# A two-layer hybrid decoder: packed weights and regrouped tiles in the last output projection, norm factors turned without a copy

## The chip, the cores and the metric

One core of one Trainium2 chip. The metric is the device time of one execution in microseconds (us), the median of three runs. The profile comes from one more execution of the same program, whose own time is given beside its span.

## The reference, cut to what matters

One sequence of 1024 positions and width 1024, a memory of 256 positions, float32 throughout. Two layers, each with one gated mixer: layer 0 is latent attention (12 heads), layer 1 an RWKV-7 recurrence (24 heads of 64), and in both four more heads attend to the memory.

```python
for layer in (mla, rwkv7):
    h = rmsnorm(x, norm_g)
    u = h @ w_in                        # queries, keys, gates ... of all heads
    mix = mixer(u)                      # 12 * 128 features
    mem_mix = memory_attention(q, *split(rmsnorm(mem, mem_norm_g) @ w_mem_kv))
    y = concat(mix, mem_mix) * silu(gate)          # 2048 features
    x = x + y @ w_out                   # the output projection
return rmsnorm(x, final_g)
```

## The kernel before

Everything lies transposed: features in the 128 partitions, positions in the columns, cut in two halves of T = 512 columns (`hf` 0 and 1). A feature tile is 128 features by 512 positions; x has 8, the gated y of a layer 16 (k 0 to 11 from the mixer, 12 to 15 from the memory heads).

Each float32 product is made of three: an operand is split into a rounded high part and the rest. For weights, `weights()` loads up to 512 columns into `wr`, ACT casts them to `wh` (L152) and DVE subtracts to get `wl` (L153); `mm3()` then issues `wh` by `yh` (L160), `wh` by `yl` (L161) and `wl` by `yh` (L162). A column of 128 weights serves one such triple. `wr`, `wh` and `wl` rotate through four buffers each; nearly all transfers are issued by SP, in order.

**Norms.** `squares()` collects the sum of squares over feature tiles in `sqa`: ACT squares (L183), DVE adds (L184). `rstd_rows()` sums over the partitions on PE (L206), which leaves one sum per position, positions in the partitions. DVE computes one over the root with whole numbers and three Newton steps on small tiles `n` (L208, L192 to L197), and a copy spreads each factor over 128 columns of `rw` (L211). `rstd_spread()` transposes `rw` on PE (L218), which puts the factor of each position into every partition, and ACT copies this from PSUM to `rstd` (L220), by which DVE multiplies the tiles. Eleven norms go this way: one for each half of x and for the two latent vectors of layer 0, one for the memory, one for each half of x at the start of layer 1 (`begin`), and the final one for each half (`finish`).

**Order.** The kernel is written with generators; `interleave()` mixes the steps of several. At build time a scheduler then sets each engine's order from its own estimates and from the buffers that are free, so an edit at one place can move instructions at others. Layer 1 runs 24 items (12 pairs of heads by two halves) through five stages; the last stage, `norm`, gives a gated y tile. The tables F0 and F1 say at which step how many tiles of the output projection of a half are woven in (`finish(0)`, `finish(1)`).

**The last output projection** is `out_proj` of layer 1 and the second half, called from `finish(1)`. It takes the y tiles in six groups, (12, 16), (0, 4), (4, 8), (8, 10), (10, 11), (11, 12), since the tiles 8 to 11 come last from the recurrence. In the first three groups each output tile m takes the group's product in PSUM and adds it to `xr` (L389). From the group (8, 10) on (`held=3`) the six output tiles m = 0 to 5 keep one PSUM bank each, in which the three last groups add up; each group loads the weights of each m by itself (256, 128 and 128 columns), 18 loads. For m = 6 and 7 nothing is done in these groups until the last, where each loads 512 columns and takes four y tiles, 12 matmuls, in the banks `c` and `y`. Behind the last group come the additions, squares, the final norm, eight multiplications (L928) and eight stores.

The y tile k=11 ends in `norm`: ACT copies it to `yT`, DVE normalises each head over its features (`m`, then `yT`, L1262), PE transposes back to a bank `y` (L1266), DVE makes `rk` and the gated `sg` (L1267, L1268), and ACT and DVE split it to `yh` and `yl` (L128, L129).

**The opening.** x is loaded, normalised and projected; `pos` gives, by `ang`, the tables of sine and cosine; the memory is normalised (`mn`), split (`mh`, `ml`) and projected to keys `mk` (copied by ACT, L271) and values. All share PE with the projections of layer 0.

## Time and profile before

| | us |
|---|---|
| runs: median (lowest to highest) | 2519.84 (2515.22 to 2521.16) |
| the profiled execution, its own time | 2510.56 |
| its span | 2508.8 |
| PE busy | 2420.2 (96%) |
| DVE busy | 1936.4 (77%) |
| ACT busy | 1375.7 (55%) |
| mean granted TensorE clock | 0.996 of full |

A busy time counts an instruction from start to end, and matmuls overlap, so what a matmul costs in a row of them is read from start to start. An idle time in brackets is time of that engine ahead of the instruction; it costs something only where the chain to the end runs through it. [...]

### The profile page before, as it was taken

How to read it: one execution, taken by the hardware profiler on the slowest of the kernel's cores; microseconds unless marked ns; L12 is line 12 of the kernel's file. 1: busy time of each engine (PE TensorE's matmuls, PEld its weight loads, DVE VectorE, ACT ScalarE, POOL GpSimd, SP SyncE). 2: the span in 40 equal slices, each digit the busy share in tenths (PEclk: the TensorE clock that was granted, in tenths of full speed). 3: DMA queues.
4: the chain of work that ended last, by engine and by line, in shares of the span. 5: the costliest groups of instructions: out<-in, count | busy, mean ns of one | idle time of the engine just before them, and what ended most of it. 6: DMA issues, size and time to landing. Idle time of an engine off the chain costs nothing.

```text
span 2508.8 us, 39875 instructions
## 1 busy us (share of the span) xinstructions
PE 2420.2 (96%) x13298; PEld 1996.1 (80%) x13298; DVE 1936.4 (77%) x5750; ACT 1375.7 (55%) x2973; POOL 55.1 (2%) x158
## 2 busy tenths in 40 slices
PE   8899999999999999999999999999999999999997
PEld 6698888888888778877778777777777777788785
DVE  7756455877787766698888888888888898786975
ACT  6445345554555334565665666666666665654542
POOL 0000000000000100000000000000000000000000
PEclk9999999999999999999999999999999999999998
DMA  5352222111112443422122222322222123222332
GB/s 178 111 171 85 76 80 74 51 56 54 49 64 68 159 168 136 143 78 76 58 73 79 80 79 78 100 82 77 79 81 80 62 84 118 87 94 98 118 137 70
DMA packets 165982, 231.45 MB, mean 92 GB/s; under 512 B 46096, under 2 KB 67984, under 8 KB 165776
## 3 DMA queue, kind: packets, MB, share of 16 engines
q1 hardware_dynamic: 165776, 228.90, 27.7%
q8 instruction: 105, 1.72, 0.3%
q14 instruction: 101, 0.83, 0.1%
HBM read 187.66 MB, written 37.49 MB: 90 GB/s over the span
## 4 chain that ended last, share of the span: by engine, by line
PE 75%; DVE 15%; ACT 6%; issue 3%; DMA 2%; SPq 0%; DVEq 0%; ACTq 0%
PE mm L160 15%; PE mm L161 15%; PE mm L162 15%; PE a L1085 3%; PE c L1218 2%; DVE tmp L1136 2%; PE pt L724 2%; DVE U L1140 2%; PE c L1221 1%; PE y L1225 1%; PE po L160 1%; PE po L161 1%; PE y L1224 1%; DVE wl L153 1%; PE po L162 1%
## 5 line engine op out<-in xcount | busy, mean ns | idle before, releaser
L152 ACT CAST wh<-wr 128x512 fp32r<-128x512 f32 (+3 forms) x500 | 299.0, 600 | 436.0 <-PE mm L161 381.0
L153 DVE TENSOR_TENSOR wl<-wr,wh 128x512 fp32r<-128x512 f32 (+3 forms) x500 | 329.6, 661 | 132.3 <-ACT wh L152 113.0
L160 PE MATMUL mm<-xnh,wh 128*128 128x512 f32 x912 | 373.9, 410 | 0.8 <-DVE qml L134 0.6
L161 PE MATMUL mm<-xnl,wh 128*128 128x512 f32 x912 | 371.2, 407 | 0.0
L162 PE MATMUL mm<-xnh,wl 128*128 128x512 f32 x912 | 369.7, 406 | 0.0
L160 PE MATMUL mm<-yh,wh 128*128 128x512 f32 x492 | 198.9, 404 | 4.3 <-DVE xr L389 4.1
L162 PE MATMUL mm<-yh,wl 128*128 128x512 f32 x492 | 196.8, 400 | 0.0
L160 PEld LDWEIGHTS mm<-xnh,wh 128*128 128x128 f32 x912 | 172.1, 189 | 30.5 <-issue 2.6
L161 PE MATMUL mm<-yl,wh 128*128 128x512 f32 x492 | 195.5, 397 | 0.0
L161 PEld LDWEIGHTS mm<-xnl,wh 128*128 128x128 f32 x912 | 172.3, 189 | 27.2 <-issue 1.4
L162 PEld LDWEIGHTS mm<-xnh,wl 128*128 128x128 f32 x912 | 172.1, 189 | 27.3 <-issue 1.0
L160 PE MATMUL mm<-xh,wh 128*128 128x512 f32 x416 | 165.2, 398 | 7.6 <-ACT xh L438 7.6
L161 PE MATMUL mm<-xl,wh 128*128 128x512 f32 x416 | 164.9, 396 | 0.6 <-DVE xl L439 0.6
L1140 DVE TENSOR_TENSOR U<-U,tmp 128x60 f32<-128x60 f32 (+24 forms) x744 | 155.9, 210 | 12.3 <-PE b L1171 0.5
L1136 DVE TENSOR_TENSOR tmp<-As,U 128x60 f32<-128x60 f32 (+24 forms) x744 | 155.6, 209 | 12.1
L162 PE MATMUL mm<-xh,wl 128*128 128x512 f32 x416 | 164.3, 395 | 0.0
L1232 ACT ACTIVATE sc<-S,f 128x128 f32<-128x128 f32 x168 | 67.4, 401 | 169.5 <-DVE S L1233 155.9
L302 ACT ACTIVATE p<-b,sm 128x512 f32<-128x512 f32 (+2 forms) x144 | 82.8, 579 | 107.3 <-DVE sm L299 82.2
L389 DVE TENSOR_TENSOR xr<-mm,xr 128x512 f32<-128x512 f32 x123 | 84.5, 688 | 67.1 <-PE mm L162 65.2
L160 PEld LDWEIGHTS mm<-yh,wh 128*128 128x128 f32 x492 | 92.7, 188 | 22.6 <-DVE xr L389 3.5
L297 DVE TENSOR_REDUCE sm<-b 128x1 f32<-128x256 f32 (+1 forms) x176 | 90.3, 527 | 24.8 <-PE b L686 10.1
L162 PEld LDWEIGHTS mm<-yh,wl 128*128 128x128 f32 x492 | 92.7, 188 | 17.0 <-issue 0.2
(361 smaller groups left out, 5968.8 us busy)
## 6 DMA issues: line engine op xcount, KB each, us to landing
wr<-in_wu_dram SPq DMA_DIRECT2D x292, 256.0 KB, 2.7
wr<-in_wo_dram SPq DMA_DIRECT2D x122, 256.0 KB, 2.6
yr<-y SPq DMA_DIRECT2D x60, 256.0 KB, 3.8
As<-sysd SPq DMA_DIRECT2D x24, 512.0 KB, 4.3
y<-y SPq DMA_DIRECT2D x32, 256.0 KB, 2.0
y<-sg SPq DMA_DIRECT2D x32, 256.0 KB, 2.0
g<-u SPq DMA_DIRECT2D x24, 256.0 KB, 2.3
gt<-g SPq DMA_DIRECT2D x24, 256.0 KB, 2.8
```

What stands on the lines that cost most here:

```text
L152: nc.scalar.copy(hi[:, :n], raw[:, :n])
L153: nc.vector.tensor_sub(lo[:, :n], raw[:, :n], hi[:, :n].bitcast(F32))
L160: mm(ps, a[0], b[0], start=start, stop=False)
L161: mm(ps, a[0], b[1], start=False, stop=False)
L162: mm(ps, a[1], b[0], start=False, stop=stop)
L297: nc.vector.tensor_reduce(sm[:, i : i + 1], ps[:, :own], AX.X, ALU.max, negate=True)
L302: nc.scalar.activation(p[:, :own], ps[:, :own], AF.Exp, bias=sm[:, 0:1], accum_out=sm[:, 2 + i : 3 + i])
L389: nc.vector.tensor_add(xs[m][:], ps[:], xs[m][:])
L1085: mm(ps[:, j * 256 : j * 256 + 256], BK[c // 4][:, c % 4, :], AR[:, c, :], start=True, stop=True)
L1136: E.tensor_tensor(out=tmp[:, 0:u, 0:n], in0=As[:, 0:u, u : u + 1].broadcast_to([P, u, n]), in1=U[:, u : u + 1, i0:8].broadcast_to([P, u, n ...
L1140: E.tensor_tensor(out=U[:, 0:u, i0:8], in0=U[:, 0:u, i0:8], in1=tmp[:, 0:u, 0:n], op=ALU.add)
L1232: ACT.activation(sc[:], cur, AF.Copy, scale=fc)
```

## The change

Three things. In the held groups `shared()` packs the weights of several output tiles into one buffer of 512 columns: two tiles for the group (8, 10), four for (10, 11) and (11, 12), with a transfer for each tile and one cast and one difference for the pack. Tiles 6 and 7 join the held groups: tile 6 begins at the group (10, 11) and tile 7 at (11, 12), each with its own load for the y tiles that came before (`before()`). `rstd_rows()` returns the small tile `n` itself, without the copy `rw`, and `rstd_spread()` transposes from one of its columns, read 128 times; with `out=False`, as in the final norm of the second half, it returns the PSUM bank, and the multiplications (now L953) read that.

```diff
@@ -38,7 +38,7 @@
 B0, S0 = 12, (10, 10)
 
 F0 = ((20, 6), (21, 2), (22, 4), (23, 10), (24, 11), (25, 11))
-F1 = ((24, 1), (25, 13), (26, 17), (27, 6))
+F1 = ((24, 1), (25, 13), (26, 17), (27, 7))
 ATT_SCALE = float(192.0 ** -0.5)
 MEM_SCALE = float(128.0 ** -0.5)
 NEG = -1.0e30
@@ -207,15 +207,15 @@
         q = self.smp.tile([P, 24], F32, tag="n", bufs=2, name=self.name("n"))
         nc.vector.tensor_scalar(q[:, 8 : 8 + n], ps[:, :n], 1.0 / width, EPS_N, ALU.mult, ALU.add)
         self.rsqrt(q, n)
-        w = self.g(s="rw")
-        nc.vector.tensor_copy(w[:, :N].rearrange("p (i t) -> p i t", t=P), q[:, 0:n:2].unsqueeze(2).broadcast_to([P, n // 2, P]))
-        return w
+        return q
 
     def rstd_spread(self, w, aux, N=T, out=None):
 
         ps = aux()
         for i in range(0, N, P):
-            self.nc.tensor.transpose(ps[:, i : i + P], w[:, i : i + P], self.ident)
+            self.nc.tensor.transpose(ps[:, i : i + P], w[:, i // 64 : i // 64 + 1].broadcast_to([P, P]), self.ident)
+        if out is False:
+            return ps
         r = out or self.g(s="rstd")
         self.nc.scalar.copy(r[:, :N], ps[:, :N])
         return r
@@ -342,7 +342,7 @@
 
 
         nc, A = self.nc, self.A
-        xs, acc, ys, kept, last = [], None, {}, [], len(groups) - 1
+        xs, acc, ys, kept, last = [], None, {}, {}, len(groups) - 1
 
         def load(g):
             raw = []
@@ -357,6 +357,32 @@
                 self.split(hi[:], lo[:], t[:])
                 ys[k] = (hi[:], lo[:])
 
+        def before(m, first, k0):
+
+            o, n = m % 2 * T + first % 4 * P, (k0 - first) * P
+            ws = self.weights(A["wo"][l, first // 4, m // 2][:, o : o + n], n)
+            self.gemm(kept[m][:], ws, [ys[k] for k in range(first, k0)], k0 - first, end=False)
+
+        pack = {}
+
+        def shared(m, k0, k1):
+
+            n = (k1 - k0) * P
+            per = min(4, T // n)
+            if (k0, m // per) not in pack:
+                raw = self.wp.tile([P, T], F32, tag="wr", name=self.name("wr"))
+                hi, lo = (self.ws.tile([P, T], F32R, tag=t, name=self.name(t)) for t in ("wh", "wl"))
+                for j in range(per):
+                    q = m // per * per + j
+                    o = q % 2 * T + k0 % 4 * P
+                    nc.sync.dma_start(raw[:, j * n : j * n + n], A["wo"][l, k0 // 4, q // 2][:, o : o + n])
+                nc.scalar.copy(hi[:], raw[:])
+                nc.vector.tensor_sub(lo[:], raw[:], hi[:].bitcast(F32))
+                pack[k0, m // per] = hi, lo
+            hi, lo = pack[k0, m // per]
+            o = m % per * n
+            return [(hi[:, o : o + n], lo[:, o : o + n])]
+
         for g, (k0, k1) in enumerate(groups):
             if k0 not in ys:
                 load(g)
@@ -367,24 +393,25 @@
                 if g == 0:
                     xs.append(self.g(s="xr"))
                     nc.sync.dma_start(xs[m][:], xin(m, hf))
-                begin, end, first = True, True, k0
-                if hold:
-                    begin, end = g == held or m >= len(held_tiles), g == last
-                    if m >= len(held_tiles):
-                        if g < last:
-                            continue
-                        first = groups[held][0]
-                n = (k1 - first) * P
-                o = m % 2 * T + first % 4 * P
-                ws = self.weights(A["wo"][l, first // 4, m // 2][:, o : o + n], n)
-                if not hold or m >= len(held_tiles):
+                begin, end = True, True
+                if not hold:
                     ps = tile()
-                elif begin:
-                    ps = held_tiles[m]()
-                    kept.append(ps)
+                    o, n = m % 2 * T + k0 % 4 * P, (k1 - k0) * P
+                    ws = self.weights(A["wo"][l, k0 // 4, m // 2][:, o : o + n], n)
                 else:
+
+                    opens = held + max(0, m - 7 + last - held)
+                    if g < opens:
+                        continue
+                    begin, end = g == opens, g == last
+                    if begin:
+                        kept[m] = held_tiles[m]()
+                        if g > held:
+                            before(m, groups[held][0], k0)
+                            begin = False
                     ps = kept[m]
-                self.gemm(ps[:], ws, [ys[k] for k in range(first, k1)], k1 - first, begin=begin, end=end)
+                    ws = shared(m, k0, k1)
+                self.gemm(ps[:], ws, [ys[k] for k in range(k0, k1)], k1 - k0, begin=begin, end=end)
                 if end:
                     nc.vector.tensor_add(xs[m][:], ps[:], xs[m][:])
                 if g == last:
@@ -916,14 +943,12 @@
                 else:
                     groups = ((12, 16), (0, 4), (4, 8), (8, 10), (10, 11), (11, 12))
                     direct = lambda k: items[NH + k]["sg"] if 8 <= k < 12 else None
-                    tiles = (self.mmt, self.mmt, x_tile, a_tile, a_tile, b_tile)
-                    rest = iter((c_tile, y_tile))
-                    turn = lambda: next(rest)() if now[0] > N + 3 else tile()
-                    yield from self.out_proj(1, hf, x1, fin, self.e, turn, groups, direct, 3, tiles)
+                    tiles = (self.mmt, self.mmt, x_tile, a_tile, a_tile, b_tile, c_tile, y_tile)
+                    yield from self.out_proj(1, hf, x1, fin, self.e, tile, groups, direct, 3, tiles)
                 w = self.rstd_rows(res[1], D, self.mmt)
                 yield
                 yield
-                r = self.rstd_spread(w, self.mmt)
+                r = self.rstd_spread(w, self.mmt, out=False if hf else None)
                 for m, x in enumerate(res[0]):
                     nc.vector.scalar_tensor_tensor(x[:], x[:], self.pc(PFG + m), r[:], ALU.mult, ALU.mult)
                     nc.sync.dma_start(A["out"][m * P : m * P + P, hf * T : hf * T + T], x[:])
```

The program keeps its PE work: 10730 rows on PE become 10732, 5620 on DVE 5599, 2455 on ACT 2437, and there are four transfers more. The order moves in several places; three matter here.

PE, the last group before: the end of tile 4's matmuls, tile 5 (bank `b`), the start of tiles 6 (`c`) and 7 (`y`). In the names `yh` and `yl` ending in 27694 and 27695 are k=11, the others k=8 and 9.

```order
L160 MATMUL a_27591<-yh_27694,wh_27750 128x512
L161 MATMUL a_27591<-yl_27695,wh_27750 128x512
L162 MATMUL a_27591<-yh_27694,wl_27751 128x512
L160 MATMUL b_27604<-yh_27694,wh_27763 128x512
L161 MATMUL b_27604<-yl_27695,wh_27763 128x512
L160 MATMUL c_27781<-yh_27436,wh_27776 128x512
L161 MATMUL c_27781<-yl_27437,wh_27776 128x512
L160 MATMUL y_27804<-yh_27436,wh_27799 128x512
L161 MATMUL y_27804<-yl_27437,wh_27799 128x512
L162 MATMUL b_27604<-yh_27694,wl_27764 128x512
```

After, the end of the last group: tile 5, tile 6 with its last triple only, and tile 7's first. `yh` and `yl` ending in 27657 and 27658 are k=11.

```order
L160 MATMUL b_27569<-yh_27657,wh_27698 128x512
L161 MATMUL b_27569<-yl_27658,wh_27698 128x512
L162 MATMUL b_27569<-yh_27657,wl_27699 128x512
L160 MATMUL c_27641<-yh_27657,wh_27698 128x512
L161 MATMUL c_27641<-yl_27658,wh_27698 128x512
L162 MATMUL c_27641<-yh_27657,wl_27699 128x512
L160 MATMUL y_27727<-yh_27416,wh_27729 128x512
L161 MATMUL y_27727<-yl_27417,wh_27729 128x512
L162 MATMUL y_27727<-yh_27416,wl_27730 128x512
L160 MATMUL y_27727<-yh_27420,wh_27729 128x512
```

Tile 5's `wl` product no longer stands behind products of other tiles; tile 6's nine matmuls with k=8 to 10 now stand ahead of the first matmul with k=11; tile 7's remain behind.

PE, the opening before: the turn of the memory's factors (`b<-cst,rw`) and its first products (`mh`, `ml`).

```order
L218 MATMUL b_1063<-cst,rw_1061 128x128 x2
L162 MATMUL mm_1227<-xh_566,wl_1196 128x512
L160 MATMUL mm_1227<-xh_573,wh_1195 128x512
L161 MATMUL mm_1227<-xl_574,wh_1195 128x512
L162 MATMUL mm_1227<-xh_573,wl_1196 128x512
L160 MATMUL mm_1271<-mh_1071,wh_1260 128x256
L160 MATMUL mm_1309<-mh_1071,wh_1298 128x256
L161 MATMUL mm_1271<-ml_1072,wh_1260 128x256
```

After, the same turn (`b<-cst,n`), and, 50 rows further on, the first products.

```order
L216 MATMUL b_1053<-cst,n_1040 128x128 x2
L160 MATMUL mm_1147<-xh_571,wh_1115 128x512
L161 MATMUL mm_1147<-xl_572,wh_1115 128x512
L162 MATMUL mm_1147<-xh_571,wl_1116 128x512
L160 MATMUL mm_1190<-xh_233,wh_1179 128x512
L161 MATMUL mm_1190<-xl_234,wh_1179 128x512
...
L161 MATMUL mm_1217<-xl_572,wh_1185 128x512
L162 MATMUL mm_1217<-xh_571,wl_1186 128x512
L160 MATMUL mm_1261<-mh_1061,wh_1250 128x256
L161 MATMUL mm_1261<-ml_1062,wh_1250 128x256
L162 MATMUL mm_1261<-mh_1061,wl_1251 128x256
```

Between turn and first product there were four matmuls; there are 51 now. Products of two heads alternated behind (`mm` 1271 and 1309); now the first head's are done before the second's.

DVE, after, the last y tile: end of the Newton steps on `m`, then `yT`, `rk`, `sg`, `yl`, and the start of the final additions.

```order
L197 SCALAR_TENSOR_TENSOR m_27576<-m_27576 128x8
L380 TENSOR_TENSOR wl_27663<-wr_27661,wh_27662 128x512
L1287 TENSOR_TENSOR yT_27165<-yT_27165,m_27576 128x512
L1292 SCALAR_TENSOR_TENSOR rk_25934<-y_27612,prm,rk_25934 128x512
L1293 SCALAR_TENSOR_TENSOR sg_25666<-rk_25934,prm,sg_25666 128x512
L380 TENSOR_TENSOR wl_27699<-wr_27697,wh_27698 128x512
L129 TENSOR_TENSOR yl_27658<-sg_25666,yh_27657 128x512
L153 TENSOR_TENSOR wl_27730<-wr_27728,wh_27729 128x384
L416 TENSOR_TENSOR xr_26495<-mm_27494,xr_26495 128x512
```

A 512-wide difference `wl` stands ahead of `yT` and one behind `sg`, where before there were differences of 128 columns, and tile 7's of 384 columns is ahead of the additions.

## Rows read from the trace of the kernel before

**Rows 1.** The page, part 1: busy us (share of the span) and instructions of each engine.
```profile
PE 2420.2 (96%) x13298; PEld 1996.1 (80%) x13298; DVE 1936.4 (77%) x5750; ACT 1375.7 (55%) x2973; POOL 55.1 (2%) x158
```
**Rows 2.** Stretches of the span: us, then busy time (x instructions) of each engine, the granted TensorE clock, DMA share, GB/s. The opening, the long middle's begin, and the last two stretches.
```profile
60.00:130.00 70.00, 60.80 (x298) 49.33 (x297) 52.71 (x123) 31.61 (x57) 0.00 (x0) 0.98 0.32 108
130.00:700.00 570.00, 566.92 (x3254) 483.40 (x3253) 372.73 (x857) 280.04 (x617) 13.92 (x60) 1.00 0.24 77
...
2440.00:2466.00 26.00, 25.76 (x141) 20.91 (x140) 13.37 (x31) 6.95 (x17) 0.00 (x0) 1.00 0.14 44
2466.00:2509.00 43.00, 24.31 (x101) 18.08 (x99) 27.11 (x68) 11.83 (x29) 0.00 (x0) 0.81 0.23 81
```
**Rows 3.** Timeline of PE from 2466 us on: start, duration, line, operation, tiles, count, and in brackets the idle time before it and what ended it. The transposes of the last y tile, the first matmul behind them, the first of the last group, the three that waited for weights, the last.
```profile
2472.70 0.63 PE L1266 MATMUL y<-cst,yT 128*128 128x128 f32 x4 [0.72 <-DVE yT L1262]
2473.08 0.48 PE L161 MATMUL mm<-yl,wh 128*128 128x512 f32 x1
...
2476.36 0.39 PE L160 MATMUL mm<-yh,wh 128*128 128x512 f32 x1
...
2481.57 0.50 PE L160 MATMUL c<-yh,wh 128*128 128x512 f32 x1 [1.03 <-ACT wh L152]
...
2483.67 0.49 PE L162 MATMUL b<-yh,wl 128*128 128x512 f32 x1 [0.73 <-DVE wl L153]
2485.55 0.79 PE L162 MATMUL c<-yh,wl 128*128 128x512 f32 x1 [1.38 <-DVE wl L153]
...
2491.61 0.39 PE L162 MATMUL y<-yh,wl 128*128 128x512 f32 x1
```
**Rows 4.** The chain that ended last, from 2466 us on: start, us, what. Pieces of the last group and the norm behind it.
```profile
2477.00 3.80 DMA wr<-in_wo_dram
...
2486.34 0.43 PE c L160
...
2489.71 0.23 PE y L162
...
2492.04 0.70 DVE xr L389
...
2494.17 1.07 PE mm L206 x8
...
2497.67 0.44 DVE rw L211
2498.15 1.13 PE mm L218 x4
2499.31 0.59 ACT rstd L220
```
**Rows 5.** Timeline of DVE from 2466 us on, columns as in rows 3: a difference of 128 columns, `rk` and `sg` of the last y tile, its `yl`, a sum of squares and an addition, two differences of 512 columns.
```profile
2469.14 0.28 DVE L153 TENSOR_TENSOR wl<-wr,wh 128x128 fp32r<-128x128 f32 x1
...
2473.37 0.75 DVE L1267 SCALAR_TENSOR_TENSOR rk<-y,prm,rk 128x512 f32<-128x512 f32 x1 [0.41 <-PE y L1266]
...
2474.23 0.74 DVE L1268 SCALAR_TENSOR_TENSOR sg<-rk,prm,sg 128x512 f32<-128x512 f32 x1
...
2475.66 0.69 DVE L129 TENSOR_TENSOR yl<-sg,yh 128x512 fp32r<-128x512 f32 x1 [0.49 <-ACT yh L128]
...
2479.43 0.69 DVE L184 TENSOR_TENSOR sqa<-sqa,sqb 128x512 f32<-128x512 f32 x1
2480.03 0.68 DVE L389 TENSOR_TENSOR xr<-a,xr 128x512 f32<-128x512 f32 x1
...
2484.81 1.28 DVE L153 TENSOR_TENSOR wl<-wr,wh 128x512 fp32r<-128x512 f32 x2
```
**Rows 6.** PE in the opening. Ahead, one row of its timeline (columns as in rows 3): the turn of the second set of norm factors. Then PE's waits between 105 and 126 us (engine, line, waited for, us in total, times, longest). Last, two stretches (columns as in rows 2).
```profile
75.11 0.63 PE L218 MATMUL b<-cst,rw 128*128 128x128 f32 x4 [1.27 <-DVE rw L211]
...
PE mm L160 <- ACT mk L271: 3.2, 1, 3.2
PE mm L160 <- ACT mh L128: 1.6, 2, 1.1
PE mm L161 <- DVE ml L129: 1.4, 4, 0.6
...
127.00:131.00 4.00, 4.00 (x23) 4.00 (x22) 3.62 (x7) 1.51 (x3) 0.00 (x0) 0.58 0.11 35
131.00:135.00 4.00, 4.00 (x36) 4.00 (x35) 3.69 (x8) 1.84 (x4) 0.00 (x0) 1.00 0.55 200
```
**Rows 7.** The opening's transfers: SP's issues (start, duration of the issues, line, tiles, count); the loads of x (KB each, median us from issue to landing, up to 130 us); and the DVE row that reads `pos`.
```profile
18.42 0.33 SPq L987 DMA_DIRECT2D w<-in_w2a_dram  x1
23.69 5.78 SPq L151 DMA_DIRECT2D wr<-in_wu_dram  x4
29.52 4.55 SPq L432 DMA_DIRECT2D x<-in_xT_dram  x8
...
120.41 1.10 SPq L493 DMA_DIRECT2D pos<-in_pos_dram  x1
...
x<-in_xT_dram SPq DMA_DIRECT2D x16, 256.0 KB, 5.6
...
124.55 0.43 DVE L495 CAST ang<-pos 128x512 f32<-128x512 int32 x1 [0.97 <-DMA pos<-in_pos_dram]
```
**Rows 8.** Timeline of PE, 924 to 942 us, columns as in rows 3: its longest wait at the start of layer 1.
```profile
937.24 0.47 PE L160 MATMUL mm<-yh,wh 128*128 128x512 f32 x1 [2.26 <-DVE xr L389]
```

## The prediction

> **What bounds the kernel now.** I read the page's busy times first: TensorE (PE) is busy 96% of the span [rows 1], so a step counts only where PE waits, or where PE is done. The table of stretches shows where: between 130 and 700 us PE is busy 566.92 of 570 us and between 2440 and 2466 us 25.76 of 26, but between 60 and 130 us only 60.80 of 70, and in the last 43 us only 24.31, with a granted clock of 0.81 [rows 2]. These two stretches hold 28 us of idle PE. All else is read inside them: the PE timeline and the chain of the last 43 us [rows 3, 4], VectorE's (DVE's) timeline beside them [rows 5], and for 60 to 130 us the list of PE's waits [rows 6].
>
> **The end, before.** The last y tile (k=11) comes from the scan; its normalisation ends with `yl` at 2475.66 + 0.69 = 2476.35 [rows 5], and PE starts the last group at 2476.36 [rows 3]. 42 matmuls are left: 3 for each of the six held tiles, 12 each for tiles 6 and 7. At the spacing of (2491.61 - 2489.71) / 8, about 0.23 us [rows 3, 4], they are 9.7 us; they take until 2491.61 + 0.39 = 2492.00, which is 15.6. The missing 6 us are three stalls on weights, 1.03 + 0.73 + 1.38 = 3.1 us [rows 3], and eight matmuls behind them at the half clock, 0.43 us apart [rows 4], after PE had idled for most of 5 us: 1.6. The rest is the slower start of each piece. The first stall hangs on a weight transfer that was issued at 2477.00 and took 3.80 us [rows 4]: it could go out only when one of four buffers was free.
>
> **The end, changed, part by part.** (1) *Packed weights*: 20 small loads become 9, so 20 casts and 20 differences become 9 each. One 512-wide difference costs 1.28 / 2 = 0.64 us, one of 128 costs 0.28 [rows 5]: four in one save 0.5 us of DVE for each pack, and as much on ScalarE (ACT). The packs need 24 transfers instead of 20, 0.33 us each on SP [rows 7], which has room for them then; hidden behind the scan's matmuls. What it costs: the order now has a 512-wide difference directly ahead of the multiplication `yT`, and a 256-wide one higher up, where two of 128 stood. That puts about 0.64 + 0.4 - 2 x 0.28 = 0.5 us into the chain of k=11. (2) *Tiles 6 and 7 in the groups*: behind k=11 there are 6 x 3 + 3 + 12 = 33 matmuls instead of 42. The nine are done earlier, while PE waits or other weights come; two matmuls move ahead of the last scan step, which is 0.46 us later. So the transposes of `yT` start at 2472.70 + 0.46 + 0.5 = 2473.7, and 52 matmuls follow: 2473.7 + 0.38 + 51 x 0.23 + 0.4 = 2486.2 for the end of the last one, if no stall is left. Is one left? The buffers of the weights of tile 7 (384 columns) come free when PE has finished tile 6's product with k=10, about 21 matmuls or 4.8 us before they are needed, and cast and difference take about 1.1 us: no. Then DVE has eight additions and seven sums of squares to do; starts are 0.60 us apart (2479.43 to 2480.03 [rows 5]). It begins at about 2479.6, behind tile 7's weights, and has eleven of them ahead of the last addition: 2486.2, just when PE ends. Addition, square and sum then take until TensorE's reduction as before, 2494.17 - 2492.04 = 2.13 us [rows 4]: 2488.4 instead of 2494.17, **-5.8 us**. Ends: with 0.69 us for each DVE step, its busy time, -4.8; with DVE never late, -6.0. (3) *Norm factors*: the copy `rw` at the end goes, 0.44 us, and the ACT copy `rstd`, 0.59 us [rows 4]: **-1.0 us**. The transposes from a broadcast column have no row before; the nearest are the same four transposes from `rw`, 1.13 us at the end [rows 4] and 0.63 at 75.11 us [rows 6]. I take the first, so no difference; the bounds are the two rows, 0.5 us either way.
>
> The eight last multiplications now read the factor from PSUM. The rows: `rk`, which reads PSUM, takes 0.75 us, and `sg`, the same form from SBUF, 0.74 [rows 5], so eight cost 0.1 us and nothing changes. [...]
>
> **The opening.** All eleven `rw` copies go, and the built order changes there. Between 105 and 126 us PE waits 1.6 us for `mh`, 1.4 for `ml` (the split of the normalised memory) and 3.2 for the copy `mk` [rows 6]. Memory is normalised and used at once: four matmuls stand between the turn of its factors and its first product. Now 51 projection matmuls, 11.7 us, stand there; the split, for whose pieces PE now waits one after the other, is then ready. The copy `mk` takes over the buffer of `pos` and so waits until DVE has read that into `ang`; `pos` went out behind weights at 120.41 and came for 124.55 [rows 7], while `mk`'s products had been done for some 3 us. That transfer now stands five places earlier on SP, some 40 matmuls ahead of the end of `mk`'s products. With these 6.2 us goes a half-clock stretch: from 127 to 131 us the granted clock is 0.58 and 23 matmuls run, in the 4 us behind it 36 [rows 6], so 4 - 23 x 4 / 36 = 1.4 us. That is -7.6. Against it: the second factor's turn (75.11, idle 1.27 [rows 6]) now has 34 matmuls for its cover where it had 42, less 0.43 for the copy, so about 1.5 us; the two others of the opening keep theirs within 0.2; mem's sum of squares still comes late, its transfers being held by the same weights. -7.0, of which I take **-6**, since the memory products now have to draw their weights at one per 12 short matmuls. Ends: 0, if such waits take it all, and -8.8. PE has no slack to eat such a gain between 130 and 700 us [rows 2], so it is kept.
>
> **The rest.** At 937.24 PE waits 2.26 us for an addition [rows 8] that the order now puts earlier, but the multiplications it passes are late next: **-1**, between 0 and -2.3. The other norms and the moved steps near 1550 and 2380 us: 0, within 1.5 either way.
>
> **Sum**: -5.8 - 1.0 - 6 - 1 = -13.8 us. The profiled execution took 2510.56 us and would take 2496.8. It lies 9.3 us under the median of the runs, 2519.84; from that I take the same 13.8: **2506 us**. 0.3% is 7.6 us, about what a measurement of this kernel can tell from no change.
>
> **Rivals.** *Only the end gains* (0.24). The opening's waits change places: a wait for weights takes that for `mk`. For it: each weight of the memory products serves only 12 short matmuls, 1.3 us; against it: in the 4 us from 131 on the same kind of work runs without a wait [rows 6]. -6.8 within 1.5: 2513 us. *The end keeps its stalls* (0.06), and the change doesn't do there what it says: packs wait for four small transfers each, and for buffers that PE frees late. For it: four buffers, of which a pack takes one for longer; against it: a pack serves 12 matmuls, where a small load served 3. Only the nine matmuls (2.1 us) and the copies come: -3.1 - 7 = -10, 2510 us, or 2517 with the rival before. *Slower* (0.08): x of the second half is loaded at 29.52 us in 4.55 us, behind four weights that went out from 23.69 [rows 7]; now it goes ahead of these, 2 MB in front of them in one queue. SP was idle there from 18.42 + 0.33 on, so I count it as free. It decides if the weights then land more than 11 us later, the work that four buffers hold (48 matmuls): PE would stand, the clock fall, and the following weights be late in turn. At twice the 5.6 us that x took to land [rows 7], with a half-clock stretch after, 11 + 7 - 6.8 = +11: 2531 us; with a few us less, no change.
>
> **How the numbers follow.** The forecast has 0.62, its own range is 2502 to 2512 (gains of 8 to 17.5). The range, **2499 to 2516**, takes in the rival of the end alone, and the runs' own scatter of 3 us. Faster by over 0.3%: the forecast but for a little (0.60), and some of the first two rivals, 0.66. Slower: half of the last rival, 0.04. Within: 0.30.
>
> **What would show it.** At the end: no idle PE over 0.3 us between the transposes of `yT` and the last matmul, the clock at 1.0 there, 33 matmuls behind `yl`, the reduction about 6 us nearer to it; no ACT instruction behind the last transposes, and the last eight at 0.67 us each. In the opening: no PE wait for `mk`, `mh`, `ml`, and 60 to 140 us shorter by 6. Wrong it would be if PE waits for `wh` or `wl` in either place, or if the last sums of squares run on long after the last matmul.

## The result and the profile after

| | before, us | after, us |
|---|---|---|
| runs: median (lowest to highest, number) | 2519.84 (2515.22 to 2521.73, 5) | 2492.78 (2490.88 to 2495.05, 5) |
| the profiled execution, its own time | 2510.56 | 2490.88 |
| its span | 2508.8 | 2489.1 |
| mean granted clock in it | 0.996 | 0.996 |

The ratio is 0.9897, with a 95% interval of 0.9882 to 0.9911: 27.1 us faster. The forecast was 2506.0 (2499 to 2516), so the direction came and the size was too small, by more than the range allowed. Between the two profiled executions lie 19.7 us, where the sum had 13.8; the other 7.4 are the 9.3 us by which the profiled execution of before lay under its median, less the 1.9 by which that of after does. These are two errors, and they have different causes. Between the same execution of before and a second one of after, shown among the experiments, lie 16.0 us. One run of the kernel before, on the chip of the last two experiments, took 2783.86 us at a mean granted clock of 0.814, and no figure here counts it.

The page of after, part 1, beside [rows 1]: PE's busy time falls by 6.2 us only, so most of the gain is waiting that went.

```profile
PE 2414.0 (97%) x13298; PEld 1995.4 (80%) x13298; DVE 1930.3 (78%) x5728; ACT 1369.4 (55%) x2957; POOL 55.3 (2%) x158
```

The stretches of after that answer to [rows 2] (same columns). From 60 to 130 us PE was busy for 60.80 us and is for 68.42, with 393 matmuls in place of 298. The next 570 us are as full as before, so nothing of this gain is lost there. The last 43 us hold 27.58 us of PE in place of 24.31.

```profile
60.00:130.00 70.00, 68.42 (x393) 59.31 (x392) 52.83 (x118) 35.78 (x68) 0.00 (x0) 1.00 0.44 143
130.00:700.00 570.00, 566.93 (x3242) 482.45 (x3240) 374.18 (x866) 279.18 (x624) 14.96 (x64) 1.00 0.23 75
2420.00:2446.00 26.00, 25.75 (x138) 20.99 (x136) 14.29 (x30) 7.62 (x16) 0.00 (x0) 1.00 0.23 72
2446.00:2489.00 43.00, 27.58 (x130) 22.25 (x128) 27.38 (x64) 10.44 (x20) 0.00 (x0) 0.83 0.19 69
```

The gain of the opening can be read at one instruction that both kernels have: the four ACT copies to `mv`, with the first and the last start before the forms. The row of before:

```profile
L284 ACT COPY mv<-mm x4: 582/587/588, 138.8 to 178.5; 128x512 f32<-128x512 f32 x4
```

And of after:

```profile
L284 ACT COPY mv<-mm x4: 582/585/590, 126.4 to 167.2; 128x512 f32<-128x512 f32 x4
```

The first starts 12.4 us sooner, the last 11.3. This is one pair of executions. In the six with after's order of the opening (two of after, four of the kernels below) the first copy starts between 126.4 and 128.9 us, in the four with before's between 138.7 and 139.6; the means lie 11.4 us apart, and 12.4 is above that. PE's timeline there shows why (idle time in brackets): a turn of norm factors, the memory's sum of squares and its turn, and the first and the 48th memory product. Of [rows 6] the three waits for `mk`, `mh` and `ml` are gone, as predicted; no weight waits took their place.

```profile
63.96 0.62 PE L216 MATMUL b<-cst,n 128*128 128x128 f32 x4 [1.21 <-DVE n L197]
...
93.45 0.58 PE L206 MATMUL b<-cst,sqa 128*128 128x2 f32 x4 [0.19 <-DVE sqa L184]
...
97.07 0.40 PE L216 MATMUL b<-cst,n 128*128 128x128 f32 x2 [0.16 <-DVE n L197]
...
108.92 0.28 PE L160 MATMUL mm<-mh,wh 128*128 128x256 f32 x1
...
114.56 0.28 PE L162 MATMUL mm<-mh,wl 128*128 128x256 f32 x1
```

Before, the same sum of squares, and the first and the 48th memory product:

```profile
106.12 0.58 PE L206 MATMUL b<-cst,sqa 128*128 128x2 f32 x4 [1.22 <-DVE sqa L184]
...
112.50 0.51 PE L160 MATMUL mm<-mh,wh 128*128 128x256 f32 x2 [1.09 <-ACT mh L128]
...
122.00 0.28 PE L162 MATMUL mm<-mh,wl 128*128 128x256 f32 x1
```

SP's issues answer to [rows 7]. x of the second half goes out at 18.43 and not at 29.52, and the weights behind it now follow from 23.34, before from 23.69: the price that the slower rival counted was not asked. The second `pos` goes out at 105.50 in place of 120.41.

```profile
18.43 3.90 SPq L459 DMA_DIRECT2D x<-in_xT_dram  x8
23.34 18.23 SPq L151 DMA_DIRECT2D wr<-in_wu_dram  x7
...
105.50 0.37 SPq L520 DMA_DIRECT2D pos<-in_pos_dram  x1
```

At the start of layer 1 the wait of [rows 8], 2.26 us, is shorter:

```profile
930.23 0.47 PE L160 MATMUL mm<-yh,wh 128*128 128x512 f32 x1 [1.29 <-DVE xr L416]
```

The end, against [rows 3]. PE's timeline of after: the transposes of the last y tile, the last matmul of the projection, the sum over the partitions and the turn.

```profile
2459.18 0.63 PE L1291 MATMUL y<-cst,yT 128*128 128x128 f32 x4 [1.00 <-DVE yT L1287]
...
2471.22 0.39 PE L162 MATMUL y<-yh,wl 128*128 128x512 f32 x1
2474.62 1.86 PE L206 MATMUL mm<-cst,sqa 128*128 128x2 f32 x8 [3.02 <-DVE sqa L184]
2478.96 1.11 PE L216 MATMUL mm<-cst,n 128*128 128x128 f32 x4 [2.47 <-DVE n L197]
```

There is no other wait between the first and the second row: the three stalls of [rows 3] are gone. DVE beside it, against [rows 5]: a packed difference ahead of `yT`, then `yl`, tile 7's difference, the first three additions, the last addition, three sums of squares behind it, and the eight multiplications from PSUM.

```profile
2457.74 0.69 DVE L380 TENSOR_TENSOR wl<-wr,wh 128x512 fp32r<-128x512 f32 x1
2458.35 0.68 DVE L1287 TENSOR_TENSOR yT<-yT,m 128x512 f32<-128x512 f32 x1
...
2462.07 0.69 DVE L129 TENSOR_TENSOR yl<-sg,yh 128x512 fp32r<-128x512 f32 x1
2463.85 0.56 DVE L153 TENSOR_TENSOR wl<-wr,wh 128x384 fp32r<-128x384 f32 x1 [1.09 <-ACT wh L152]
2464.85 2.05 DVE L416 TENSOR_TENSOR xr<-mm,xr 128x512 f32<-128x512 f32 x3 [0.44 <-PE mm L162]
...
2471.69 0.69 DVE L416 TENSOR_TENSOR xr<-y,xr 128x512 f32<-128x512 f32 x1
2472.29 2.28 DVE L184 TENSOR_TENSOR sqa<-sqa,sqb 128x512 f32<-128x512 f32 x3
...
2480.11 5.36 DVE L953 SCALAR_TENSOR_TENSOR xr<-xr,prm,mm 128x512 f32<-128x512 f32 x8 [1.21 <-PE mm L216]
```

Counted from the start of the last step of the scan (PE's last `y<-SAV,AM`, at 2466.34 before and 2452.11 after), in us:

| kernel | turn of `yT` | `yl` | last matmul | L206 | turn of factors | end of span |
|---|---|---|---|---|---|---|
| before | 6.36 | 9.32 | 25.27 | 27.83 | 31.81 | 42.44 |
| after | 7.07 | 9.96 | 19.11 | 22.51 | 26.85 | 36.99 |

The end gave 5.5 us of the 19.7, all that lies ahead of it 14.2.

### The profile page after: what moved, and what is told of

It reads as the page before. It is cut to its first block, busy times and chain, and to the rows that moved or that the text cites. A ratio compares the mean times of both kernels' runs of the same rounds, so it can differ in the third digit from the quotient of the medians.

```text
span 2489.1 us, 39834 instructions
## 1 busy us (share of the span) xinstructions
PE 2414.0 (97%) x13298; PEld 1995.4 (80%) x13298; DVE 1930.3 (78%) x5728; ACT 1369.4 (55%) x2957; POOL 55.3 (2%) x158
## 4 chain that ended last, share of the span: by engine, by line
PE 74%; DVE 15%; ACT 6%; issue 2%; DMA 2%; SPq 0%; DVEq 0%; ACTq 0%
PE mm L160 15%; PE mm L161 15%; PE mm L162 15%; PE a L1110 3%; PE c L1243 2%; DVE tmp L1161 2%; PE pt L751 2%; PE c L1246 2%; DVE U L1165 1%; PE y L1250 1%; PE po L160 1%; PE po L161 1%; DVE wl L153 1%; PE y L1249 1%; PE po L162 1%
## 5 line engine op out<-in xcount | busy, mean ns | idle before, releaser
L152 ACT CAST wh<-wr 128x512 fp32r<-128x512 f32 (+2 forms) x482 | 293.1, 609 | 407.0 <-PE mm L161 351.3
L153 DVE TENSOR_TENSOR wl<-wr,wh 128x512 fp32r<-128x512 f32 (+2 forms) x482 | 324.3, 674 | 130.5 <-ACT wh L152 111.1
L161 PEld LDWEIGHTS mm<-xnl,wh 128*128 128x128 f32 x912 | 172.3, 189 | 27.1 <-issue 1.4
```

The costliest lines, as they stand in the source:

```text
L152: nc.scalar.copy(hi[:, :n], raw[:, :n])
L153: nc.vector.tensor_sub(lo[:, :n], raw[:, :n], hi[:, :n].bitcast(F32))
L161: mm(ps, a[0], b[1], start=False, stop=False)
```

## The experiments

Two questions: what in the opening and the rest gave 14.2 us where 7 were reckoned, and what at the end is worth how much. All medians stand beside runs of the kernel before on the same chip (2517.35 for the first four, 2518.66 for the next four, 2520.0 for the last two).

**The kernel before, again** (no edit). Why is the profiled execution so far under the median?

> The kernel before, once more, to see where its runs (2515 to 2522 us) lose the 5 to 11 us that its profiled execution (2510.56) did not lose. Theory (clock): more of its stalls end in a stretch at the half clock, each 3.4 us long and worth 1.7 us; then the slower runs show a lower mean granted clock, about 0.990 to 0.993 against 0.996, and a profile near 2519 us has four or five such stretches more than one near 2510. Rival (transfers): the clock is 0.996 in all runs and the time goes into waits for transfers, above all in the opening and at the end. Time: 2515 to 2522 us, ratio 1.000.

Measured: 2518.15 (11 runs), ratio 1.0001 (0.9991 to 1.0012). This time the profiled execution took 2520.53 us, at a mean clock of 0.992. Two stretches show the difference, first in the profile that the prediction read (columns as in [rows 2]).

```profile
833.00:838.00 5.00, 5.00 (x39) 4.58 (x39) 2.61 (x5) 1.66 (x3) 0.02 (x1) 1.00 0.62 200
939.00:944.00 5.00, 5.00 (x24) 4.13 (x23) 5.00 (x8) 2.43 (x5) 0.00 (x0) 1.00 0.96 315
```

Then the same stretches in this one:

```profile
833.00:838.00 5.00, 5.00 (x29) 4.92 (x28) 1.76 (x4) 1.07 (x2) 0.86 (x4) 0.66 0.57 188
939.00:944.00 5.00, 4.55 (x13) 3.63 (x14) 3.52 (x6) 0.95 (x3) 0.00 (x0) 0.66 0.97 296
```

From 833 to 838 us one execution ran 39 matmuls at full clock (1.00), the other 29 at 0.66; from 939 to 944 it is 24 and 13. A mean of 0.66 over 5 us is 3.4 us at the half clock; from 836.4 to 837.4 us the second profile has 0.50, and 1.00 behind it. The wait ahead of 833 us is the same in both. PE's row in the first:

```profile
831.70 0.36 PE L160 MATMUL po<-pth,vh 128*128 128x256 f32 x1 [2.69 <-DVE y L738]
```

And in the second:

```profile
832.54 0.35 PE L160 MATMUL po<-pth,vh 128*128 128x256 f32 x1 [2.70 <-DVE y L738]
```

So a wait of 2.7 us is followed by a half-clock stretch in one execution and not in another. This execution has such stretches near 114 (0.66 from 113 to 118 us), 127 (memory products 0.21 us apart, 0.12 behind it), 834, 940, 2373 (0.52 from 2373 to 2383 us) and 2496 us (matmuls 0.43 us apart); the first had them near 127 (0.58 [rows 6]) and at the end only. Both run the same program, so the loss can be read from the starts of the same matmuls: of the 9.9 us between the spans 0.7 are lost near 114, 1.5 near 834, 1.7 near 940 and 5.0 near 2373, where the half clock lasts 10 us behind a wait of 1.61 us (1.02 in the first execution); another 0.8 near 1106 go without half clock. Over 51 runs of before, the medians by mean clock are 2510.7 us at 0.996 (2 runs), 2514.2 at 0.995 (11), 2516.4 at 0.994 (12), 2519.6 at 0.993 (17) and 2520.3 at 0.992 (8), with one run of 2524.2 at 0.991: 2.4 us for each 0.001. Only two of the 51 were about as fast as the profiled execution of the prediction.

**The norms alone**, on the kernel before (the copy `rstd` stays):

```diff
-        w = self.g(s="rw")
-        nc.vector.tensor_copy(w[:, :N]..., q[:, 0:n:2]...broadcast_to([P, n // 2, P]))
-        return w
+        return q
...
-            self.nc.tensor.transpose(ps[:, i : i + P], w[:, i : i + P], self.ident)
+            self.nc.tensor.transpose(ps[:, i : i + P], w[:, i // 64 : i // 64 + 1].broadcast_to([P, P]), self.ident)
```

> Before, with the norm factors turned without the copy rw alone (the ACT copy rstd stays, the output projection is as before). Its order on PE and DVE is the changed kernel's up to the last 90 rows. Theory 1 (the order of the opening pays, and the scatter of the runs hangs on the stalls there): -14 us of span ahead of the end, 0.4 at the end, and the runs lose their scatter: 2499 to 2501 us, ratio 0.992. Theory 2 (the scatter hangs on the stalls at the end): -14.5, 2505 us, ratio 0.994. Theory 3 (opening worth only the 7 us of the rows): 2512 us.

Measured: 2497.14 (2494.96 to 2501.53), ratio 0.9921 (0.9908 to 0.9934), -20.2 us. `mv` starts at 127.2, that is -11.6. At the end the waits on weights stay (0.76, 0.31, 0.73 and 1.38 us), and the span ends 41.97 us after the last scan step.

**The output projection alone**, on the kernel before: this line, and the change's edits in `out_proj` and of `tiles` in `finish`.

```diff
-F1 = ((24, 1), (25, 13), (26, 17), (27, 6))
+F1 = ((24, 1), (25, 13), (26, 17), (27, 7))
...
```

> Before, with the new output projection alone (packs, tiles 6 and 7 in the groups); copies rw and rstd stay. Its order is that of before up to the last 90 rows. Theory 1: the end gains 4 to 4.5 us (5.5 in the changed kernel less rw and rstd), 2515 us, ratio 0.998, scatter as before. Theory 2 (scatter from the end): -4.5 - 7, 2508 us, ratio 0.9955. Theory 3: as predicted, -5.8 us.

Measured: 2513.37 (2507.78 to 2519.68, 11 runs), ratio 0.9984 (0.9975 to 0.9993), -4.0 us. The end takes 37.98 us from the scan step, -4.5, and `mv` starts at 138.9, as before. The scatter of before, 12 us, stays as well. The two parts add up to 24.2 us, the whole change to 27.1 on its first chip and 25.4 on another (below): within the scatter, neither part needs the other.

**The copy back, but unread.** After, with DVE still making `rw` while PE turns the small tile:

```diff
         self.rsqrt(q, n)
+        w = self.g(s="rw")
+        nc.vector.tensor_copy(w[:, :N]..., q[:, 0:n:2]...broadcast_to([P, n // 2, P]))
         return q
```

> The changed kernel, with the copy rw made by DVE but not read by anyone: the transposes still read the small tile. Its opening has nearly the order of before (122 PE rows differ from before, 296 from the changed kernel). Theory A (the order pays): the opening's gain of 12.4 us is gone but for the copies out of the chain, 3 times 0.4 us; the end gains 5.5: 2513 us, ratio 0.9975. Theory B (the shorter chain from sum to transposes pays): as the changed kernel, within 2 us: 2495 us, ratio 0.990.

Measured: 2507.39 (2503.72 to 2511.58), ratio 0.9961 (0.9948 to 0.9973); `mv` starts at 135.8, -3.0 where the whole change has -12.4. Against before on the same chip that is -10.0 us, between theory A (-6.3 by its ratio) and theory B (-25), nearer to A. The chain is as short as in after; what came back is the order. The scheduler counts the copy's DVE time, and places the turn of the memory's factors 6 rows ahead of the first memory product, where before has 4 and after has 51. PE's waits from 100 to 140 us:

```profile
105.29 0.58 PE L206 MATMUL b<-cst,sqa 128*128 128x2 f32 x4 [0.80 <-DVE sqa L184]
...
111.75 0.50 PE L160 MATMUL mm<-mh,wh 128*128 128x256 f32 x2 [1.04 <-ACT mh L128]
112.70 0.39 PE L161 MATMUL mm<-ml,wh 128*128 128x256 f32 x1 [0.45 <-DVE ml L129]
...
116.89 0.50 PE L160 MATMUL mm<-mh,wh 128*128 128x256 f32 x2 [0.52 <-ACT mh L128]
...
123.96 0.38 PE L160 MATMUL mm<-mh,wh 128*128 128x256 f32 x1 [2.63 <-ACT mk L273]
```

They are the three waits of [rows 6], 2.63 us for `mk` among them. So most of the opening's gain is an order that the scheduler happened upon when the copy left its sums, and little of it is the copy's 0.43 us. Of the 3.0 us that stayed some 1.4, as the prediction reckoned it, are the half-clock stretch at 127 us, which this execution does not have: its memory products stay 0.12 us apart behind the wait for `mk`.

**The copy back in four of the eleven norms** (one latent vector, the memory, one half in `begin`, the last), and read there:

```diff
+        self.calls = getattr(self, 'calls', 0) + 1
+        if self.calls in (3, 5, 8, 11):
+            w = self.g(s="rw")
+            nc.vector.tensor_copy(w[:, :N]..., q[:, 0:n:2]...broadcast_to([P, n // 2, P]))
+            self.wides[id(w)] = w
+            return w
         return q
...
```

> The changed kernel, with the copy rw put back and read in four of the eleven norms: one latent norm and the memory's in the opening, the first half's at the start of layer 1, and the last one. Its order on PE differs from the changed kernel's in 8 rows. Theory A (the order of the opening pays, the copies next to nothing): 0.4 us at the end, 0.4 each at the two turns of the opening that still wait (idle 1.21 and 0.16), nothing in layer 1: +1.0 us, 2494 us, ratio 0.990. Theory B (the copies in the chains pay): four of the five chains are long again, so most of the opening's gain goes: 2502 us or more.

Measured: 2497.28 (2495.06 to 2499.86), ratio 0.9923 (0.9909 to 0.9936). The order is after's (49 rows between the turn and the first memory product), and `mv` starts at 127.4, within the 126.4 to 128.9 us of the executions with this order and no copy: read the other way round, copies on the same chains cost little as long as the order holds. That supports the last experiment. Over the two medians of after (2492.78 and, below, 2494.59) 2.7 to 4.5 us are lost in all, more than expected; 1.0 of them is at the start of layer 1, where the wait is back to what it was in [rows 8]:

```profile
926.78 0.47 PE L161 MATMUL mm<-yh,wh 128*128 128x512 f32 x1 [2.31 <-DVE xr L423]
```

The rest stays open.

**Joining without packs.** After, but each of the eight held tiles loads its own weights:

```diff
-                    ws = shared(m, k0, k1)
+                    o, n = m % 2 * T + k0 % 4 * P, (k1 - k0) * P
+                    ws = self.weights(A["wo"][l, k0 // 4, m // 2][:, o : o + n], n)
```

> The changed kernel without packs: tiles 6 and 7 are in the groups, each tile loads its own 256 or 128 columns. Packs pay (theory 1): ACT and DVE have 18 small splits in place of 7 large, DVE comes later to the additions and PE waits for wh or wl between the last triples: +2 to +3 us, 2495 us. Packs cost (theory 2): the 512-wide differences ahead of yT and in front of yl go, the transposes of yT start 0.5 us earlier: -0.5 us, 2492 us. Against before ratio 0.989 to 0.991 in both; the profile's end decides.

Measured: 2499.96 (2498.66 to 2500.71), ratio 0.9929 (0.9916 to 0.9941). The end takes 41.62 us from the scan step, 4.6 more than in after and only 0.8 less than before, about what the missing copies `rw` and `rstd` are worth. The stalls on weights are there:

```profile
2472.48 0.50 PE L160 MATMUL y<-yh,wh 128*128 128x512 f32 x1 [0.63 <-ACT wh L152]
...
2475.03 0.50 PE L162 MATMUL b<-yh,wl 128*128 128x512 f32 x1 [1.58 <-DVE wl L153]
2476.50 0.50 PE L162 MATMUL c<-yh,wl 128*128 128x512 f32 x1 [0.98 <-DVE wl L153]
```

**Packs without joining.** Before, with packs for tiles 0 to 5; 6 and 7 come late as before, and both copies stay:

```diff
-                ws = self.weights(A["wo"][l, first // 4, m // 2][:, o : o + n], n)
+                if hold and m < len(held_tiles):
+                    ws = shared(m, k0, k1)
+                else:
+                    ws = self.weights(A["wo"][l, first // 4, m // 2][:, o : o + n], n)
```

> Before, with packs for tiles 0 to 5 alone (also for the two columns that tiles 6 and 7 would use, unused); tiles 6 and 7 wait for the last group as before, norms with both copies. Theory 1: the stalls on weights at the end go (3.1 us and the half clock behind them, 1.6), 42 matmuls stay: -3 to -4 us. Theory 2: tiles 6 and 7 cause the stalls, since their two loads of 512 columns come last and have four buffers to share with the packs: 0 to -1 us, and joining them is what pays.

Measured: 2508.01 (2506.01 to 2511.16), ratio 0.9964 (0.9952 to 0.9977), -10.7 us. The end takes 36.88 us, -5.6, with 42 matmuls in the last group and not 33 (two of tile 6 stand ahead of the first with k=11), and with both copies. The other 5.1 us between the medians are not located: the projection alone, with the same order ahead of the end, gained 4.0 in all. The last matmul starts 19.26 us after the scan step (after: 19.11), L206 22.05 (after: 22.51). PE's timeline, the turn of `yT`, the last matmul and L206:

```profile
2479.19 0.63 PE L1289 MATMUL y<-cst,yT 128*128 128x128 f32 x4 [1.01 <-DVE yT L1285]
...
2491.12 0.39 PE L162 MATMUL y<-yh,wl 128*128 128x512 f32 x1
2493.91 1.17 PE L206 MATMUL mm<-cst,sqa 128*128 128x2 f32 x8 [2.40 <-DVE sqa L184]
```

From the turn of `yT` to the last matmul PE takes 11.93 us here and 12.04 in after: the matmuls that joining takes out of the last group stand ahead of it, behind the turn, where PE is as busy. So the packs are the whole gain of the projection at the end, and the joining none. DVE here, the first three additions, three sums of squares and the last addition:

```profile
2483.60 1.89 DVE L412 TENSOR_TENSOR xr<-mm,xr 128x512 f32<-128x512 f32 x3 [0.22 <-PE mm L162]
...
2489.60 2.27 DVE L184 TENSOR_TENSOR sqa<-sqa,sqb 128x512 f32<-128x512 f32 x3
2491.78 0.68 DVE L412 TENSOR_TENSOR xr<-y,xr 128x512 f32<-128x512 f32 x1
```

The additions begin 11.74 us after the scan step, in after 12.74, since there PE does tile 6's nine matmuls ahead of the last group. So here one sum of squares is left behind the last addition, and in after three.

**Useless matmuls behind the last product.** In after L206 took 1.86 us, at a granted clock of 0.50, before 1.07 [rows 4] at 1.00, and PE had idled 3.02 us ahead of it. Twelve products that nobody reads keep PE at work there:

```diff
+                if warm and g == last and m == 7:
+                    junk = warm()
+                    for _ in range(12):
+                        nc.tensor.matmul(junk[:], ws[0][0][:, :P], ys[k0][0], start=True, stop=True)
```

> The changed kernel with 12 matmuls of no use behind the last product (into a free bank, 12 x 0.227 = 2.7 us), while PE waits 3.0 us for the last sums of squares. Clock theory: the reduction and the turn at the end run at the full clock, 1.05 us or less in place of 1.86 and 0.63 in place of 1.11: -0.8 to -1.3 us at the end. Rival (the two are slow for another reason): no change, or + 0.2 for the fill of PE's queue.

Measured: 2493.46 (2493.12 to 2493.96), ratio 0.9904 (0.9891 to 0.9918): no gain beside 2492.78 and 2494.59 of after. L206 does take 1.05 us, but so it does in another execution of after itself (the next section), behind the same 3.02 us; behind 3.0 us it took 1.55, 1.67 and 1.82 in three other kernels with joined tiles. The turn takes 1.11 us, as in after, where its clock is 0.50, and not 0.63: PE waits 2.48 us ahead of it all the same. This profile also waits 4.62 us near 821 us, where after waits 2.71, so the medians can't tell a gain of under 1 us. PE with the twelve products, 2.88 us or 0.16 more than 12 x 0.227, where 0.29 us are left to wait:

```profile
2474.50 2.88 PE L423 MATMUL b<-yh,wh 128*128 128x512 f32 x12
2477.67 1.05 PE L206 MATMUL mm<-cst,sqa 128*128 128x2 f32 x8 [0.29 <-DVE sqa L184]
```

PE in the other execution of after:

```profile
2479.14 1.05 PE L206 MATMUL mm<-cst,sqa 128*128 128x2 f32 x8 [3.02 <-DVE sqa L184]
2482.67 1.12 PE L216 MATMUL mm<-cst,n 128*128 128x128 f32 x4 [2.47 <-DVE n L197]
```

**Packs and norms without joining**, and **after, again**, on one chip, against the change as it is: packs for tiles 0 to 5 as two experiments above, and the norm factors as in after.

```diff
-            self.nc.tensor.transpose(ps[:, i : i + P], w[:, i : i + P], self.ident)
+            self.nc.tensor.transpose(ps[:, i : i + P], w[:, i // 64 : i // 64 + 1].broadcast_to([P, P]), self.ident)
+        if out is False:
+            return ps
...
-                r = self.rstd_spread(w, self.mmt)
+                r = self.rstd_spread(w, self.mmt, out=False if hf else None)
```

> The changed kernel without its second part: packs for tiles 0 to 5, tiles 6 and 7 wait for the last group as before, norm factors without copies. Its order up to the last 60 rows of PE is the changed kernel's. Theory 1 (packs make the whole gain at the end, joining nothing): from the last scan step to the end 36.9 us with packs alone and both copies, less 0.44 and 0.59 for the copies: 35.8 against 37.0 in the changed kernel, so 1.1 us faster than it, 2491 to 2492 us. Theory 2 (joining pays once the copies are gone): +1 to +2 us, 2494 us.

> The changed kernel once more, beside the one without joined tiles, and to see its scatter: one stall is left that ends in a half-clock stretch (2.7 us near 819 us), so runs should lie within 2490 to 2496 us at a granted clock of 0.996 to 0.998, half the scatter of before. Ratio 0.989 to 0.991.

Measured: without joining 2492.09 (2489.80 to 2492.91), ratio 0.9890 (0.9872 to 0.9907); after again 2494.59 (2492.07 to 2495.72), ratio 0.9899 (0.9881 to 0.9917). The ends take 35.73 and 36.18 us from the scan step. L206 without joining:

```profile
2477.46 1.05 PE L206 MATMUL mm<-cst,sqa 128*128 128x2 f32 x8 [2.40 <-DVE sqa L184]
```

It starts 22.05 us after the scan step, as with packs alone; in the six profiles with packs and joined tiles it starts at 22.5 to 22.6. So joining is not only worth nothing, it costs some 0.5 us there, and up to 0.8 more: behind the longer wait, 3.02 us, L206 took 1.86 us at a clock of 0.50 in one execution of after and 1.05 in the other. The 2.5 us between the medians are no more than the runs scatter.

## Why the prediction was right or wrong

**From which execution the gain is subtracted: wrong, 7.4 us.** The prediction saw that its profile lay 9.3 us under the median and wrote "from that I take the same 13.8". That step holds only if the 9.3 us are time that the change doesn't touch. They were mostly half-clock stretches, which the second execution of before has in four places where the first had none: near 114, 834, 940 and 2373 us. The change takes away the first of these waits and about halves the third, so the usual execution gains more than the profiled one. The second stays (2.71 us near 819), and after's own profile has a half-clock stretch behind it (granted clock 0.72 from 819 to 825 us); the fourth stays too (1.02 us before, 1.06 after). The stretch near 940 us, worth some 1.7, stands in three of the four profiles with before's order ahead of the end and in none of the six with after's; that near 834 (819 in after) in three of the four and five of the six; those near 114 and 2373 in one of the four. So some 1.7 us of the 7.4 are shown to go with a wait that the change shortened, and where the rest goes stays open. After's profile lies only 1.9 us under its median.

**The opening: mechanism right, 6 taken, 12.4 measured (11.4 between the means).** The waits for `mk`, `mh` and `ml` went with the order, and so did the half-clock stretch at 127 us (in after the granted clock is 1.00 from 126 to 131 us). Three terms were mis-sized. (a) Stalls were priced by the idle time in brackets, which begins at the modelled end of the matmul before, 0.28 us behind its start for a memory product, where they start 0.12 us apart in a row. Start to start they cost more: before, the first 48 memory products spread from 112.50 to 122.00 us, after from 108.92 to 114.56, so 3.9 us, of which the brackets show 1.9 ([rows 6], 1.6 + 1.4 less the 1.09 ahead of the first). (b) "Mem's sum of squares still comes late": that wait, 1.22 us, fell to 0.19 in this execution, but in the five others with this order it is 0.28 to 1.42, so part of the 12.4 is luck. The second factor's turn did not grow to 1.5 but waits 1.21; by the prediction's own terms, eight matmuls less for its cover and one copy less, it would have been 1.27 + 8 x 0.23 - 0.43 = 2.7. The order on DVE changed as well: from the sum over the partitions to this turn there are 10.0 us now and were 12.0. (c) The 1 us held back for weights was not needed. Added up, 1.1 for the first product, 3.9, 3.4 for `mk`, 1.4 for the clock and 1.2 for sum and turns are 11.0. Of the other 1.4 us 0.8 lie ahead of the first turn of factors (28.90 us, before 29.71), which starts between 28.90 and 29.82 in the six executions with this order; 0.6 are not located. The experiment with the unread copy shows the cause: with nearly before's order 9.4 of the 12.4 are gone.

**The rest: -1 taken, about right at its place.** At the start of layer 1 the timelines gain 1.6 us. Near 1550 us, where 0 was taken within 1.5, it is -2.0, and near 1740 -0.6; behind the wait of 819 us, and near 1100, after's execution lost 1.2 us each to before's.

**The end: -6.8 taken with the copies (-7.3 from the last scan step, which the prediction put 0.46 us later), -5.5 measured.** The packs were right: every stall on weights and the half clock behind them went (granted clock 1.00 from the turn of `yT` to the last matmul). Wrong was the credit for the nine matmuls "done earlier, while PE waits": packs alone bring the last matmul to 19.26 us, packs with joining to 19.11. The step that failed in the sum is the one behind it. DVE has, as reckoned, eleven of its fifteen additions and sums ahead of the last addition; then four are left, that addition and three sums of squares, and they were priced as "addition, square and sum" with one. Without joining only one sum is left there, and joining, which puts the additions 1.0 us later, leaves three. From the last addition to L206 it takes 2474.62 - 2471.69 = 2.93 us, not 2.13, and L206 comes 22.51 us after the scan step, not 21.6. The other 0.8 us is L206 itself, 1.86 us and not 1.05, in this one execution: in the second execution of after it takes 1.05, and the end 36.18.

**The norm factors at the end: right.** The turn takes 1.11 us, as before, and the copies `rw` and `rstd` are out of the chain. The multiplications from PSUM take 5.36 us for eight, against 5.39 from `rstd` in SBUF before:

```profile
2499.93 5.39 DVE L928 SCALAR_TENSOR_TENSOR xr<-xr,prm,rstd 128x512 f32<-128x512 f32 x8 [1.83 <-ACT rstd L220]
```

So reading the factor from PSUM cost these eight nothing that the two traces show, as the prediction took it from `rk` and `sg`.

**The rivals.** Only the end gains: refuted by the opening. The end keeps its stalls: refuted in after, and seen in the kernel that joins without packs. Slower by x ahead of weights: SP was free there, as the prediction counted, and the weights went out as early as before.

## What to carry to other kernels

Before a gain is taken from a median, ask how far the profiled execution lies from it and in which places; if it is clock behind waits that the change removes, the usual execution gains that as well. Read the gain at a place from more than one execution of each kernel: the opening's ranged over 2.5 us with the same order. Price a stall from start to start against the spacing of undisturbed work, not by the idle time alone. Where a scheduler sets the order, an edit is worth what it does to the order, and the trial that tells is one that keeps the operation in the scheduler's sums and takes it out of the data's way.

## What the runs showed of the hardware

The same wait ends at full clock in one execution and in half clock in another: 2.69 and 2.70 us near 832 us, 39 and 29 matmuls in the same 5 us behind them, at 1.00 and 0.66; and 3.02 us ahead of L206 in after, 1.86 us for the eight reductions in one execution, at 0.50, and 1.05 in another. The 51 runs of the kernel before beside the experiments lie between 2510.6 and 2524.2, their medians in the order of their mean clocks. The ten runs of after, on two chips, lie closer, between 2490.88 and 2495.72.
